# Column blocks of the input projection in parts of the tokens, with the convolution taken from the PSUM bank

## The chip, the cores and the metric

One core of a Trainium2 chip runs the whole layer as one program. The metric is the device time of one execution in microseconds. TensorE (PE) multiplies, VectorE (DVE), ScalarE (ACT) and GpSimd (POOL) do the elementwise work, SyncE (SP) issues most of the DMAs. Each engine takes its instructions in the order in which the program gives them; engines wait for each other by semaphores.

## The reference, cut to what matters

A layer normalises 1024 latent tokens (a grid of 16 rows by 64) and 256 context tokens, multiplies them by one input projection, and feeds the columns to a gated DeltaNet in two directions (queries, keys and values behind a short convolution) and to a pooling mixer. An output projection and a mixture of 16 experts follow. The part that the change touches:

```python
def short_conv(x, w):
    C = x.shape[-1]
    return lax.conv_general_dilated(
        x, w[:, None, :], window_strides=(1,),
        padding=[(CONV_K // 2, CONV_K - 1 - CONV_K // 2)],
        dimension_numbers=('NWC', 'WIO', 'NWC'), feature_group_count=C)
...
    proj = h @ w_in
    (q, k, v), log_a, beta = deltanet_inputs(proj[..., :QKV_COLS], proj[..., QKV_COLS:STATE_COLS],
                                             conv_w, a_log, dt_bias)
...
    feats = jax.nn.silu(short_conv(feat_pre, conv_w))
```

CONV_K is 4: token t of a channel sums tokens t-2, t-1, t and t+1 with weights 0 to 3, and tokens outside the sequence count as zero. Keys and values are computed for the context as well, queries, gates and pooled columns for the latent tokens alone.

## The kernel before

The projection is computed transposed, channels on the 128 partitions and tokens along the free axis, in column blocks of 128 channels: four key blocks, four value blocks, eight blocks that alternate between pooling and queries in the order PQ, four gate blocks. Inputs and weights are split into a high and a low float32r part (hx, hc for the tokens, whi, wlo for the weights), so that each k (8 slices of the 1024 inputs) takes three matmuls per tile. A block has the tiles px0 and px1 (512 latent tokens each, one PSUM bank each) and, for keys and values, pc (256 context tokens). Each of the names has one buffer in the PSUM pool PS2.

`project_steps` is a generator: for each k it issues the matmuls of all tiles of the block (six of 512 columns, and three of 256 with the context) and yields, eight times per block. At k = 1 it calls `prefetch`, which splits the next block's weights (ACT writes whi at L200, DVE or POOL writes wlo at L201; the first four on DVE) and has SP load the raw weights of the block after (L193, one buffer `wraw`).

After the block's last k a generator of its own, a post, is put into the list `posts`. `advance_posts` moves every post by one step. For keys, values and queries the post is `conv_post` (L407): in its first step ACT and DVE copy the PSUM tiles into `pad` and `padc` in SBUF; then ACT multiplies by the weight of tap 0 (L424) and, a step apart each, DVE adds the three other taps over all 1024 tokens (`scalar_tensor_tensor`, L428). The context's four taps follow in one step (L431, L433), then both Silus, and some steps later PE transposes the result in groups of four tiles of 128 tokens (L446). For keys ACT copies the group into `rows` and SP stores it (Kd); for values DVE scales it into `rows` (L463) and SP stores it (Vd). `rows` has one buffer, and so has `vT`, which holds a value block, a pooling block's input or, at first, the columns of a and beta.

The first key block is built while its inputs are still being modulated (L517 to L539); the three others run in a loop over `ks` (L584) that moves the posts and one step of the remaining small products of the modulation vector (`mg`, PE L132, fed by the DMA of `wm`) after each yield. The state of ten token chunks is then prepared by `prep` (L629), two chunks at a time, while values, queries, pooling and gates are projected: `run` (L782) calls `advance_preps` and `advance_posts` after each yield of the projection. A prep begins when every key block is through its transposes (`k_left`). It is a chain of small matmuls and short operations of DVE and ACT: kk (L663), eight products with the decays on DVE (L666), four transposes (L672), a first product on PE (L675), four rounds of PE (L687), DVE (L679, L683) and ACT (L681), then the joining of blocks (L700 to L743). Its masks are made by POOL, which also does the sums of the pooling posts (L821, L828). The scan over the chunks (`scan`, PE sc L923) begins when the projection and the last prep are through.

Of the kernel before, what the change touches and what calls it, by code (L numbers as in the profile page):

```python
# [52 lines left out]
def trunk_kernel(ctx, tc, x, c, ctxt, c_ctx, w_mod, b_mod, norm1, norm2, w_in, conv_w, a_log, dt_bias,  # L53
# [262 lines left out]
    def token_groups(n):  # L316
        return [(g, min(4, n - g)) for g in range(0, n, 4)]
# [88 lines left out]

    def conv_post(ct, px, pc, dst, after):  # L407

        pad = CV.tile([128, L + 4], F32, name="pad")
        acc = CV.tile([128, L], F32, name="acc")  # L410
        DVE.memset(pad[:, 0:2], 0.0)
        DVE.memset(pad[:, L + 2:L + 4], 0.0)
        for t in range(2):
            copy2(t, pad[:, 2 + 512 * t:514 + 512 * t], px[t])
        o = 0
        if pc is not None:
            padc = CV.tile([128, LC + 4], F32, name="padc")
            accc = CV.tile([128, LC], F32, name="accc")
            DVE.memset(padc[:, 0:2], 0.0)
            DVE.memset(padc[:, LC + 2:LC + 4], 0.0)  # L420
            ACT.activation(padc[:, 2:2 + LC], pc, AF.Copy)
            o = LC
        yield
        ACT.activation(acc, pad[:, 0:L], AF.Copy, scale=convw(0, ct))  # L424
        for j in range(1, 4):
            for _ in range(1):
                yield
            DVE.scalar_tensor_tensor(acc, pad[:, j:j + L], convw(j, ct), acc, op0=OP.mult, op1=OP.add)  # L428
        yield
        if pc is not None:  # L430
            DVE.tensor_scalar(accc, padc[:, 0:LC], convw(0, ct), None, op0=OP.mult)  # L431
            for j in range(1, 4):
                DVE.scalar_tensor_tensor(accc, padc[:, j:j + LC], convw(j, ct), accc, op0=OP.mult, op1=OP.add)  # L433
            ACT.activation(dst[:, 0:LC], accc, AF.Silu)
        ACT.activation(dst[:, o:o + L], acc, AF.Silu)
        yield
        for _ in range((1, 1, 0)[ct // 4]):
            yield
        n = (o + L) // 128
        tp = None  # L440
        for g, m in token_groups(n):
            if tp is not None:
                after(tp, *last)
            tp, last = rows_tile(ct, g // 4), (g, m)
            for q in range(m):
                PE.transpose(tp[:, q, :], dst[:, 128 * (g + q):128 * (g + q) + 128], ident)  # L446
            yield
        after(tp, *last)

    def k_sumsq(h):  # L450
        def f(tp, g, m):
            rows = CV.tile([128, 4, 128], F32, name="rows", bufs=1)
            ACT.activation(rows[:, :m], tp[:, :m], AF.Copy)
            SP.dma_start(Kd[g:g + m, :, h, :].rearrange("t p c -> p t c"), rows[:, :m])
            ACT.activation(tp[:, :m], tp[:, :m], AF.Square)
            DVE.tensor_reduce(ssk[:, g:g + m, h], tp[:, :m], axis=AX.X, op=OP.add)
            k_left[0] -= m
        return f

    def v_rows(h):  # L460
        def f(tp, g, m):
            rows = CV.tile([128, 4, 128], F32, name="rows", bufs=1)
# [13 lines left out]

    def project_tiles(with_ctx):
        return [(PS2.tile([128, 512], F32, name=f"px{t}"), hx, slice(512 * t, 512 * t + 512)) for t in range(2)] + \
            ([(PS2.tile([128, 512], F32, name="pc")[:, 0:LC], hc, slice(0, LC))] if with_ctx else [])

# [4 lines left out]

    def project_steps(n, with_ctx, post):
        for h in range(n):
            done[0] += 1
            hi, lo = split.pop(done[0] - 1)
            px = project_tiles(with_ctx)  # L490
            for k in range(KD):
                if k == 1:
                    prefetch()
                project_mm(px, k, ((hi, 0), (hi, 1), (lo, 0)), k == 0, k == KD - 1)
                if k == KD - 1:
                    posts.append(post(h, *project_out(px)))
                yield

    def project_out(px):
        return [p[0] for p in px[0:2]], px[2][0] if len(px) > 2 else None  # L500

# [4 lines left out]

    k_post = lambda h, px, pc: conv_post(4 + h, px, pc, kT[:, h, :], k_sumsq(h))
    mg = more_gemv()
    done[0] += 1
    hi, lo = split.pop(0)  # L510
    px = project_tiles(True)

# [27 lines left out]
    prefetch()  # L540
    first = project_out(px)
    ks = project_steps(H - 1, True, lambda h, px, pc: k_post(h + 1, px, pc))
    px, pc = ab_px[0:2], ab_px[2]
# [19 lines left out]
    def ab_post(px, pc):  # L563
        abT = CV.tile([128, LC + L], F32, name="vT")
        ACT.activation(abT[:, 0:LC], pc, AF.Copy)
# [15 lines left out]
    advance_posts()  # L581
    posts.append(k_post(0, *first))
    advance_posts()
# [205 lines left out]
    def v_post(h, px, pc):  # L789
        vT[0] = CV.tile([128, LC + L], F32, name="vT")  # L790
        return conv_post(8 + h, px, pc, vT[0], v_rows(h))

# [8 lines left out]

    def pool_post(g, px):

        w = 2 << g
        hw = w // 2
        wid = GRID + w
        u = CV.tile([128, LC + L], F32, name="vT").rearrange("p (r c) -> p r c", r=ROWS)
        s = PL.tile([128, ROWS + 16, GRID + 16], F32, name="psum_c")
        POOL.memset(u[:, :, 0:hw], 0.0)
        POOL.memset(u[:, :, hw + GRID:wid], 0.0)  # L810
        for t in range(2):
            copy2(t, u[:, 8 * t:8 * t + 8, hw:hw + GRID], px[t].rearrange("p (r c) -> p r c", c=GRID))
        POOL.memset(s[:, 0:hw, 0:GRID], 0.0)
# [34 lines left out]

    def gate_post(h, px):
        st = CV.tile([128, L + 4], F32, name="pad")[:, 0:L]  # L850
        for t in range(2):
            ACT.activation(st[:, 512 * t:512 * t + 512], px[t], AF.Silu)
        for _ in range(1):
            yield
        DVE.tensor_scalar(st, st, prmT[:, R_DN:R_DN + 1], None, op0=OP.mult)
        fp_store(h, st)

    def q_post(h, px):
        return conv_post(h, px, None, qT[:, h, :], q_sumsq(h))

    run(project_steps(2 * H, False,
                      lambda i, px, pc: (pool_post if PQ[i][0] == "p" else q_post)(PQ[i][1], px)))
    run(project_steps(H, False, lambda h, px, pc: gate_post(h, px)))
    while posts or todo or active:
# [986 lines left out]
```

## Time and profile before

| | us |
|---|---|
| time before, median of 3 runs | 1363.76 (1360.57 to 1364.97) |
| the profiled execution | 1365.92 |
| its span on the core | 1364.2 |
| PE busy | 1261.2 (92%) |
| DVE busy | 1029.5 (75%) |
| ACT busy | 751.1 (55%) |
| POOL busy | 390.6 (29%) |

The key blocks after the first take about us 69 to 140 of the span, the values to 234, queries and pooling to 430, the gates to 491. The scan, the output projection and the routing follow to about 782, the experts to the end. PE's busy time counts pipelined matmuls whose ends are modelled, so it doesn't show how many of them there could have been; its idle time, and what ended it, is a safer reading. An idle time in brackets stands at the instruction that ended it, with its releaser.

### The profile page before, as it was taken

Reading aid. Unit: us, or ns where it says so; the run is one execution under the profiler, and the core shown is the slowest. Engines: PE = TensorE matmul, PEld = TensorE weight load, DVE = VectorE, ACT = ScalarE, POOL = GpSimd, SP = SyncE. Lnnn points to the kernel's source line nnn. Section 1 sums busy time; section 2 is a strip of 40 time slices with the busy share of each in tenths; the row PEclk is TensorE's granted clock in tenths of the full one; section 3 lists DMA queues with packets and bytes.
Section 4 is the critical chain, followed back from the end, with each engine's and each line's share of the span. In section 5 each row is a group of like instructions: output and inputs, shape, how many; then the busy total and the mean of one; then the engine's idle time right before and its main releaser. Section 6 shows DMA issues by size and latency. Waiting matters only on the chain.

```text
span 1364.2 us, 26631 instructions
## 1 busy us (share of the span) xinstructions
PE 1261.2 (92%) x10355; PEld 1003.4 (74%) x10355; DVE 1029.5 (75%) x1773; ACT 751.1 (55%) x1103; POOL 390.6 (29%) x394
## 2 busy tenths in 40 slices
PE   5899889989999989989982799999999999999997
PEld 3476777666767779978872688888888888888884
DVE  4763665675775436864659699999999999999995
ACT  5443434343433324333233477777777777777783
POOL 5700552494865113761116000000000000000002
PEclk9999989998999989999995799999999999999999
DMA  9667213212123268634686599999999999999806
GB/s 353 209 193 276 70 37 91 86 49 79 49 79 95 87 221 317 214 128 154 231 322 232 188 340 369 386 385 384 379 383 382 388 381 385 383 382 383 298 4 259
DMA packets 140760, 328.39 MB, mean 241 GB/s; under 512 B 13517, under 2 KB 53082, under 8 KB 140634
## 3 DMA queue, kind: packets, MB, share of 16 engines
q1 hardware_dynamic: 134826, 305.72, 60.8%
q0 software_dynamic: 5376, 19.40, 5.6%
q8 instruction: 81, 1.33, 0.4%
q10 hardware_dynamic: 432, 1.57, 0.3%
q14 instruction: 45, 0.37, 0.1%
HBM read 287.32 MB, written 39.32 MB: 239 GB/s over the span
## 4 chain that ended last, share of the span: by engine, by line
PE 75%; DVE 11%; issue 4%; POOL 4%; DMA 3%; ACT 2%; SPq 0%; POOLq 0%; ACTq 0%; DVEq 0%
PE pg L1638 14%; PE pu L1638 13%; PE pd L1638 12%; PE px L484 11%; PE y L1256 6%; PE sc L923 5%; PE iv L687 2%; DVE acc L428 2%; PE tp L1674 2%; PE gv L132 1%; DMA wm<-in_w_mod_dram 1%; DVE pT L666 1%; DMA Vd<-rows 1%; PE pc L484 1%; DVE T L704 1%
## 5 line engine op out<-in xcount | busy, mean ns | idle before, releaser
L484 PE MATMUL px<-hx,whi 128*128 128x512 f32 x640 | 222.0, 427 | 4.6 <-ACT hx L290 2.7
L1516 DVE TENSOR_TENSOR flo<-rawb,fhi 128x1024 fp32r<-128x1024 f32 x176 | 208.6, 1224 | 11.2 <-ACT fhi L1515 10.5
L1515 ACT ACTIVATE fhi<-rawb 128x1024 fp32r<-128x1024 f32 x176 | 186.1, 1062 | 53.6 <-PE pg L1638 19.0
L1516 DVE TENSOR_TENSOR flo<-rawa,fhi 128x1024 fp32r<-128x1024 f32 x158 | 187.3, 1224 | 12.9 <-ACT fhi L1515 12.2
L1515 ACT ACTIVATE fhi<-rawa 128x1024 fp32r<-128x1024 f32 x158 | 167.2, 1062 | 51.3 <-PE pg L1638 21.9
L1638 PE MATMUL pg<-fhi,lhs 128*128 128x512 f32 x544 | 157.9, 402 | 0.0
L1638 PE MATMUL pu<-fhi,lhs 128*128 128x512 f32 x512 | 146.6, 398 | 0.0
L484 PEld LDWEIGHTS px<-hx,whi 128*128 128x128 f32 x640 | 113.2, 193 | 40.5 <-issue 12.4
L1744 POOL DMA_INDIRECT accd<-ye,ix x15 | 34.6, 2310 | 366.2 <-DVE ye L1742 366.2
L1638 PE MATMUL pd<-fhi,lhs 128*128 128x512 f32 x480 | 134.2, 396 | 0.0
L484 PE MATMUL px<-hx,wlo 128*128 128x512 f32 x320 | 128.5, 402 | 0.0
L1638 PEld LDWEIGHTS pg<-fhi,lhs 128*128 128x128 f32 x544 | 100.8, 190 | 22.6 <-ACT lhs L1676 0.4
L1638 PEld LDWEIGHTS pu<-fhi,lhs 128*128 128x128 f32 x512 | 95.1, 188 | 21.8
L1638 PEld LDWEIGHTS pd<-fhi,lhs 128*128 128x128 f32 x480 | 90.1, 188 | 21.6
L1638 PE MATMUL pg<-flo,lhs 128*128 128x512 f32 x272 | 86.2, 398 | 0.0
L1638 PE MATMUL pu<-flo,lhs 128*128 128x512 f32 x256 | 80.5, 395 | 0.0
L1256 PE MATMUL y<-ohi,mx 128*128 128x512 f32 x256 | 76.4, 404 | 0.8 <-DVE oa L981 0.8
L201 POOL TENSOR_TENSOR wlo<-wraw,whi 128x1024 fp32r<-128x1024 f32 x16 | 41.1, 2568 | 125.2 <-ACT whi L200 125.2
L1638 PE MATMUL pd<-flo,lhs 128*128 128x512 f32 x240 | 75.5, 396 | 0.0
L484 PEld LDWEIGHTS px<-hx,wlo 128*128 128x128 f32 x320 | 61.6, 193 | 14.0
L428 DVE SCALAR_TENSOR_TENSOR acc<-pad,prmT,acc 128x1024 f32<-128x1024 f32 x36 | 66.3, 1843 | 3.6 <-ACT acc L424 3.3
L1664 POOL DMA_INDIRECT xe<-h2d,ix x16 | 16.4, 1027 | 168.7 <-PE pg L1638 120.7
(453 smaller groups left out, 2405.1 us busy)
## 6 DMA issues: line engine op xcount, KB each, us to landing
rawb<-in_w_down_dram SPq DMA_DIRECT2D x61, 512.0 KB, 6.1
rawb<-in_w_gate_dram SPq DMA_DIRECT2D x58, 512.0 KB, 5.1
rawb<-in_w_up_dram SPq DMA_DIRECT2D x57, 512.0 KB, 6.0
rawa<-in_w_gate_dram SPq DMA_DIRECT2D x56, 512.0 KB, 5.0
rawa<-in_w_up_dram SPq DMA_DIRECT2D x54, 512.0 KB, 6.1
rawa<-in_w_down_dram SPq DMA_DIRECT2D x52, 512.0 KB, 6.1
wm<-in_w_mod_dram SPq DMA_DIRECT2D x48, 512.0 KB, 5.7
wraw<-in_w_in_dram SPq DMA_DIRECT2D x20, 512.0 KB, 4.1
```

Source lines behind the costliest of these rows:

```text
L201: (POOL if pos[0] > 4 else DVE).tensor_tensor(lo[:, :, :n], raw[:, :, :n], hi[:, :, :n].bitcast(F32), op=OP.subtract)
L428: DVE.scalar_tensor_tensor(acc, pad[:, j:j + L], convw(j, ct), acc, op0=OP.mult, op1=OP.add)
L484: PE.matmul(dst, wp[:, k, :], src[hp][:, k, o], start=start and i == 0, stop=stop and i == len(parts) - 1)
L687: PE.matmul(iv[r, u, o:64], pa[r, u, :], PV[r, u, o:64], start=True, stop=True)
L923: PE.matmul(p[:, h, :], lhs(h), rhs(h), start=True, stop=True)
L1256: PE.matmul(ys[t, hf][:, hf, :], l_[:, k, :], r_[:, 512 * hf:512 * hf + 512], start=(k == KORD[0] and i == 0), stop=(k == KORD[-1] and i = ...
L1515: ACT.activation(hi, raw, AF.Copy)
L1516: (eng or DVE).tensor_tensor(lo, raw, hi.bitcast(F32), op=OP.subtract)
L1638: PE.matmul(ps[:, hf, :], l_[:, k, :], r_[:, 512 * hf:512 * hf + 512], start=(k == 0 and n == 0), stop=(k == KD - 1 and n == 2))
L1664: POOL.indirect_dma_start(out=xe[e], out_offset=None, in_=h2d[:, :], in_offset=bass.IndirectOffsetOnAxis(ap=ix[:, 0:1], axis=0))
L1674: PE.transpose(tp[:, q, :], src[:, 128 * k:128 * k + 128], ident)
L1744: POOL.indirect_dma_start(out=accd[:, :], out_offset=bass.IndirectOffsetOnAxis(ap=idx.pop(e)[:, 0:1], axis=0), in_=ye, in_offset=None, com ...
```

## The change

A block is now computed part after part: context (for keys and values), then the first 512 latent tokens, then the second, each over all eight k before the next part begins. The tile `px` has two buffers, which the parts take in turn. A part of 512 tokens yields four times, after six matmuls each; the context part yields twice, after twelve. A block with the context therefore has ten steps where it had eight.

Each part has its own post, put into the list after its last k. `conv_part` does the convolution without the copies: ACT writes tap 2 from the PSUM tile to the place of the result, and DVE adds the taps 0, 1 and 3 in place, reading the same PSUM tile, a step apart (the context's three in one step). The two tokens at the seam between the parts get a small operation of their own. The PSUM tile is free when tap 3 is done. `pad`, `acc`, `padc` and `accc` go; one Silu in place takes context and latent tokens together. `rows` and `vT` get two buffers. The posts of pooling and gates take parts as well; the gates write to a tile `gt`.

```diff
-    def conv_post(ct, px, pc, dst, after):
...
+    def conv_part(ct, acc, b, ps):
+
+        n, e = ps.shape[1], acc.shape[1]
+        h = 2 if b else 0
+        if b + n < e:
+            DVE.memset(acc[:, b + n:b + n + 2], 0.0)
+        ACT.activation(acc[:, b + h:b + n], ps[:, h:n], AF.Copy, scale=convw(2, ct))
+        if h:
+            DVE.scalar_tensor_tensor(acc[:, b:b + 2], ps[:, 0:2], convw(2, ct), acc[:, b:b + 2], op0=OP.mult, op1=OP.add)
+        for j in (0, 1, 3):
+            if n > LC or j == 0:
                 yield
-            DVE.scalar_tensor_tensor(acc, pad[:, j:j + L], convw(j, ct), acc, op0=OP.mult, op1=OP.add)
-        yield
...
+            t0, t1 = max(b + 2 - j, 0), min(b + n + 2 - j, e)
+            DVE.scalar_tensor_tensor(acc[:, t0:t1], ps[:, t0 + j - 2 - b:t1 + j - 2 - b], convw(j, ct), acc[:, t0:t1],
+                                     op0=OP.mult, op1=OP.add)
+        yield
+
+    def conv_post(ct, dst, after, part, ps):
+
+        n = dst.shape[1]
+        o = n - L
+        if part == "c":
+            yield from conv_part(ct, dst[:, 0:LC], 0, ps)
+            return
+        yield from conv_part(ct, dst[:, o:n], 512 * part, ps)
+        if part == 0:
+            return
+        ACT.activation(dst, dst, AF.Silu)
         yield
...
-            rows = CV.tile([128, 4, 128], F32, name="rows", bufs=1)
+            rows = CV.tile([128, 4, 128], F32, name="rows", bufs=2)
...
+    def project_tile(part):
+        if part == "c":
+            return PS2.tile([128, 512], F32, name="pc")[:, 0:LC], hc, slice(0, LC)
+        return PS2.tile([128, 512], F32, name="px", bufs=2), hx, slice(512 * part, 512 * part + 512)
...
+            for part in ("c", 0, 1)[0 if with_ctx else 1:]:
+                tile = project_tile(part)
+                for k in range(KD):
+                    if k == 1 and part == ("c" if with_ctx else 0):
+                        prefetch()
+                    project_mm([tile], k, ((hi, 0), (hi, 1), (lo, 0)), k == 0, k == KD - 1)
+                    if k == KD - 1:
+                        posts.append(post(h, part, tile[0]))
+                    if k % 4 == 3 or part != "c" and k % 2:
+                        yield
...
-    px = project_tiles(True)
+    px = [project_tile(part) for part in (0, 1, "c")]
...
-    posts.append(k_post(0, *first))
+    for part, ps in zip((0, 1, "c"), first):
+        posts.append(k_post(0, part, ps))
...
+        if part == "c":
+            vT[0] = CV.tile([128, LC + L], F32, name="vT", bufs=2)
+        return conv_post(8 + h, vT[0], v_rows(h), part, ps)
...
+    def gate_post(h, part, ps):
+        if part == 0:
+            gate_t[h] = CV.tile([128, L], F32, name="gt")
+        st = gate_t[h]
+        ACT.activation(st[:, 512 * part:512 * part + 512], ps, AF.Silu)
+        yield
+        if part == 0:
+            return
```

## Rows read from the trace of the kernel before

**Rows 1.** Busy time by stage; the first row names the columns.

```profile
core 0: us, PE busy (x) PEld busy (x) DVE busy (x) ACT busy (x) POOL busy (x), PEclk, DMA share, GB/s
...
69.00:140.00 71.00, 69.86 (x421) 47.70 (x420) 33.44 (x92) 30.44 (x51) 6.69 (x6) 1.00 0.67 225
...
140.00:234.00 94.00, 84.75 (x1151) 71.50 (x1150) 60.79 (x126) 36.83 (x64) 41.01 (x31) 0.95 0.22 65
...
234.00:430.00 196.00, 183.78 (x3144) 138.71 (x3142) 127.72 (x260) 75.01 (x144) 125.72 (x92) 0.95 0.24 73
```

**Rows 2.** Waits, us 140 to 491: waiter, releaser, us in total, times, longest.

```profile
PE iv L675 <- DVE PV L672: 8.0, 7, 5.7
...
PE iv L728 <- DVE T L722: 7.0, 4, 2.8
...
PE iv L687 <- DVE PV L683: 4.6, 5, 1.9
...
PE iv L728 <- ACT T L731: 1.3, 1, 1.3
...
PE iv L700 <- DVE PV L692: 0.2, 1, 0.2
...
ACT vT L434 <- DVE accc L433: 18.5, 3, 11.7
```

**Rows 3.** One source line each: count, ns min/median/max, first and last start.

```profile
L428 DVE SCALAR_TENSOR_TENSOR acc<-pad,prmT,acc x36: 1272/1285/4329, 76.4 to 400.7; 128x1024 f32<-128x1024 f32 x36
...
L666 DVE SCALAR_TENSOR_TENSOR pT<-dt,nbt,pT x80: 335/341/351, 170.3 to 465.4; 128x128 f32<-128x128 f32 x80
...
L1780 DVE SCALAR_TENSOR_TENSOR ye<-pg,af,g2b x2: 741/746/750, 1336.8 to 1337.5; 128x512 f32<-128x512 f32 x2
...
L433 DVE SCALAR_TENSOR_TENSOR accc<-padc,prmT,accc x24: 483/485/488, 82.4 to 249.5; 128x256 f32<-128x256 f32 x24
```

**Rows 4.** Timeline: start us, duration, engine, operation, idle time in brackets.

```profile
166.31 4.08 DVE L428 SCALAR_TENSOR_TENSOR acc<-pad,prmT,acc 128x1024 f32<-128x1024 f32 x2
...
173.07 0.68 PE L675 MATMUL iv<-PV,pT 32*32 32x32 f32 x4 [5.71 <-DVE PV L672]
...
278.57 17.61 POOL L828 TENSOR_TENSOR psum_c<-psum_c 128x1984 f32<-128x1984 f32 x4
...
279.83 4.33 DVE L428 SCALAR_TENSOR_TENSOR acc<-pad,prmT,acc 128x1024 f32<-128x1024 f32 x1 [1.64 <-ACT acc L424]
```

**Rows 5.** Timeline of DVE and PE at the last value block.

```profile
238.30 0.42 DVE L463 TENSOR_TENSOR rows<-tp,nrk 128x256 f32<-128x256 f32 x1 [3.38 <-DMA Vd<-rows]
...
241.25 0.93 PE L728 MATMUL iv<-T,pT 64*64 64x64 f32 x16 [2.80 <-DVE T L722]
```

**Rows 6.** First of five low-clock windows, and their sum; columns as in Rows 1.

```profile
170.50:180.70 10.20, 7.22 (x137) 5.83 (x137) 6.21 (x18) 1.64 (x3) 7.53 (x2) 0.50 0.01 3
...
sum 30.70, PE 27.00 PEld 18.87 DVE 20.94 ACT 5.22 POOL 12.44; mean PE 5.40 PEld 3.77 DVE 4.19 ACT 1.04 POOL 2.49
```

**Rows 7.** From the first key block to the second: timelines, landing of wraw.

```profile
66.78 9.72 SPq L193 DMA_DIRECT2D wraw<-in_w_in_dram  x2
...
DMA to landing us min/median/max: 3.9/3.9/3.9
...
68.78 0.39 ACT L421 ACTIVATE padc<-pc 128x256 f32<-128x256 f32 x1 [0.78 <-PE pc L484]
...
74.88 1.22 DVE L201 TENSOR_TENSOR wlo<-wraw,whi 128x1024 fp32r<-128x1024 f32 x1 [5.23 <-ACT whi L200]
```

**Rows 8.** Waits of PEld, 69 to 140; chain of waits, 142 to 150.

```profile
PEld gv L132 <- DMA wm<-in_w_mod_dram: 5.3, 6, 1.2
...
146.94 1.40 PE px L484 x6
```

**Rows 9.** Timeline at the end of the projection.

```profile
492.14 1.36 POOL L890 DMA_DIRECT2D v<-Vd  x2 [17.59 <-PE iv L728]
...
495.79 2.05 PE L923 MATMUL sc<-v,T 128*128 128x128 f32 x8 [0.43 <-DMA v<-Vd]
```

More of the change, by code (lines that the diff above doesn't have):

```diff
@@ L438, in conv_post @@
             yield
-        n = (o + L) // 128
         tp = None
-        for g, m in token_groups(n):
+        for g, m in token_groups(n // 128):
             if tp is not None:
@@ L461, in f @@
         def f(tp, g, m):
-            rows = CV.tile([128, 4, 128], F32, name="rows", bufs=1)
+            rows = CV.tile([128, 4, 128], F32, name="rows", bufs=2)
             DVE.tensor_tensor(rows[:, :m], tp[:, :m], nrk[:, g:g + m, h:h + 1].to_broadcast([128, m, 128]),
@@ L540, in trunk_kernel @@
     prefetch()
-    first = project_out(px)
-    ks = project_steps(H - 1, True, lambda h, px, pc: k_post(h + 1, px, pc))
+    first = [p[0] for p in px]
+    ks = project_steps(H - 1, True, lambda h, part, ps: k_post(h + 1, part, ps))
     px, pc = ab_px[0:2], ab_px[2]
@@ L563, in ab_post @@
     def ab_post(px, pc):
[L564 removed]
+        abT = CV.tile([128, LC + L], F32, name="vT", bufs=2)
         ACT.activation(abT[:, 0:LC], pc, AF.Copy)
@@ L787, in trunk_kernel, with v_post @@
     vT = [None]
-    def v_post(h, px, pc):
-        vT[0] = CV.tile([128, LC + L], F32, name="vT")
-        return conv_post(8 + h, px, pc, vT[0], v_rows(h))
+    def v_post(h, part, ps):
+        if part == "c":
+            vT[0] = CV.tile([128, LC + L], F32, name="vT", bufs=2)
+        return conv_post(8 + h, vT[0], v_rows(h), part, ps)
     run(project_steps(H, True, v_post))
@@ L800, in fp_store, with pool_post @@
         SP.dma_start(fpd[:, :, i, :].rearrange("t p c -> p t c"), src.rearrange("p (t c) -> p t c", c=128))
-    def pool_post(g, px):
+    pool_u = {}
+    def pool_post(g, part, ps):
         w = 2 << g
@@ L806, in pool_post @@
         wid = GRID + w
-        u = CV.tile([128, LC + L], F32, name="vT").rearrange("p (r c) -> p r c", r=ROWS)
+        if part == 0:
+            pool_u[g] = CV.tile([128, LC + L], F32, name="vT", bufs=2).rearrange("p (r c) -> p r c", r=ROWS)
+            POOL.memset(pool_u[g][:, :, 0:hw], 0.0)
+            POOL.memset(pool_u[g][:, :, hw + GRID:wid], 0.0)
+        u = pool_u[g]
+        copy2(part, u[:, 8 * part:8 * part + 8, hw:hw + GRID], ps.rearrange("p (r c) -> p r c", c=GRID))
+        if part == 0:
+            return
         s = PL.tile([128, ROWS + 16, GRID + 16], F32, name="psum_c")
[L809 to L812, printed above, removed]
         POOL.memset(s[:, 0:hw, 0:GRID], 0.0)
@@ L847, in pool_post, with q_post @@
         fp_store(H + g, m)
[L849 to L854, printed above, removed]
+    gate_t = {}
+    def gate_post(h, part, ps):
+        if part == 0:
+            gate_t[h] = CV.tile([128, L], F32, name="gt")
+        st = gate_t[h]
+        ACT.activation(st[:, 512 * part:512 * part + 512], ps, AF.Silu)
+        yield
+        if part == 0:
+            return
         DVE.tensor_scalar(st, st, prmT[:, R_DN:R_DN + 1], None, op0=OP.mult)
         fp_store(h, st)
-    def q_post(h, px):
-        return conv_post(h, px, None, qT[:, h, :], q_sumsq(h))
+    def q_post(h, part, ps):
+        return conv_post(h, qT[:, h, :], q_sumsq(h), part, ps)
     run(project_steps(2 * H, False,
-                      lambda i, px, pc: (pool_post if PQ[i][0] == "p" else q_post)(PQ[i][1], px)))
-    run(project_steps(H, False, lambda h, px, pc: gate_post(h, px)))
+                      lambda i, part, ps: (pool_post if PQ[i][0] == "p" else q_post)(PQ[i][1], part, ps)))
+    run(project_steps(H, False, gate_post))
     while posts or todo or active:
```

39 lines of the change are left out of this document (1 added, 38 removed).

## The prediction

> **What bounds the kernel now.** I read the profile in this order: busy time by stage, to see where the changed code runs; the waits of PE in that stretch; the instructions that PE waited for; then what had delayed those.
>
> The changed code runs from us 69 to 491. PE is taken as busy nearly all of the key stage, 69.9 of 71 us, and is idle more in the two stages behind it, 9.3 of 94 us and 12.2 of 196 us [rows 1]. So no matmul is saved by the change, and none is: what it can give back are waits. In us 140 to 491 PE waited 23.3 us in nine groups; the first four are 20.9 us, the last is 0.2 us, and all four are first matmuls of a prep step that wait for DVE or ACT [rows 2]. The matmuls of the projection themselves wait for almost nothing: between the end of a block and the next stand prep matmuls that hide the copies.
>
> What had delayed DVE is the convolution. A tap over 1024 tokens takes 1.285 us at the median and up to 4.33 us [rows 3]. The long ones lie beside POOL: the tap at 279.83 took 4.33 us while POOL ran four sums from 278.57 on [rows 4]. Two taps from 166.31 on take 4.08 us, where two medians are 2.57, and behind them PE idles 5.71 us for the first prep [rows 4]. DVE's 80 operations of the same kind that read one operand from PSUM run in the same stretch and never leave 335 to 351 ns [rows 3]. So it is the pair DVE and POOL, both on SBUF, that is slow, not the operation.
>
> Two more costs follow. With the single `rows` DVE waits for the store of the group before: 3.38 us at 238.30, behind which PE idles 2.80 us [rows 5]. And five stretches between us 170 and 410, 30.7 us in all, run at a granted clock of 0.50, which is the 1.2 GHz level; the first begins in the 5.71 us idle time. PE is busy 27.0 us of them [rows 6], so at 2.4 GHz it would have needed about 13.5 us less.
>
> **The change part by part.** The sum is made against the profiled execution: 1365.9 us, of which the span is 1364.2 and 1.7 lie around it; the median of the runs is 2.2 us lower.
>
> *Taps from PSUM.* Removed are 36 taps of 1024 tokens, the copies and the separate tap 0; added are 72 taps of 512. The nearest row is the same operation of 512 elements from PSUM late in the kernel: 746 ns [rows 3]. Six of them are 4.48 us per block, where three old ones are 3.86 us at the median and 12.99 us at the worst [rows 3]. So DVE has no less work where POOL is quiet; the gain is that a queue of 1.3 to 4.3 us in front of a prep step becomes 0.75 us. Taken wait by wait [rows 2]: the first prep's 5.7 us had 4.08 us of taps ahead of it and keeps one of 0.75, so 3.3 go. Of the 4.6 us of the rounds (L687) nearly all lies behind single long taps: 4.0 go. The 1.3 us for ACT comes of a Silu that waited in ACT's queue for the context's taps; ACT waited 18.5 us in all for those, which now end a part earlier: 1.0 goes. Of the other 2.3 us of L675 1.0 goes, of the 4.2 us of L728 that are not the store's 1.4, of the 2.4 us of small ones 1.2. Sum: 11.9 us. It can't be more than the 20.5 us that are not the store's. It can be nothing if the prep's own chain, eight decay products and four transposes, is what is late next.
>
> The Trainium skill speaks against this part: "VectorE: DVE Perf Modes", section "Rules for kernel authors", has a kernel that does many operations on a matmul's output copy it to SBUF first. By it the old form would be the right one, and two taps of 0.746 against one of 1.285 us [rows 3] agree with it as long as POOL is quiet; what it would make of the time is the second rival.
>
> *Two buffers for rows and vT.* The wait of 2.80 us [rows 5] nearly goes: 2.5 us. SP's queue has the same stores in the same order, none is added.
>
> *The clock.* If the idle times in front of the stretches shrink, the stretches do. Of the 13.5 us I take 9, the share of the waits that go, with 0 and 13.5 as ends.
>
> *The first key block.* Here the change adds a wait. All three parts of that block go into `posts` together, and the second block now begins with its context part, whose tile pc has one buffer: its first matmul waits until the context's taps of the first block are done. In DVE's queue stand in front of these: the split of the third block's low weights (`prefetch` is now issued before the posts move), one reduction, and one tap of each part of 512. The split waits for ACT, and ACT for `wraw`, which SP issues at 66.78 and which lands 3.9 us later, at 70.7 [rows 7]. From there: about 1.0 us of ACT for whi, 1.22 us for wlo [rows 7], about 0.4 for the reduction, 2 x 0.746, and 3 taps of 256 at 0.485 or so [rows 3]: 5.5 us, so 76.2. PE is ready when the old copy of the context begins, 68.78 [rows 7]. Queued behind that matmul on PE are the transposes of a and beta and the small products: nothing else can run, and PE idles about 7 us (4 to 9). After the 5.71 us idle time PE ran at half speed for several us [rows 4, 6]; I take 4 us for that. The first latent part then waits for tap 3 of the first block, behind the reductions that need those transposes: 2 us more. Against these 13 us stands that the small products have waited up to 5.3 us for their weights [rows 8], whose loads go on meanwhile: 4 us come back. Net 9 us lost, with 3 and 15 as ends.
>
> *Steps.* Blocks with context have ten steps for eight. A step of six matmuls is 1.40 us [rows 8], so twelve of 256 columns are about as long. The four value blocks give the preps eight steps more, and the first prep begins one step earlier, so the preps end some nine steps ahead of the last matmul. Today the load of the first scan's `v`, issued on POOL's queue, waits for the last prep (492.14) and the scan for that load (495.79) [rows 9]. I take 2 us for it, 0 to 5: SP's loads for the second chunk stay where they are.
>
> *A PSUM tile that is held longer.* Until tap 3 is done, three steps after ACT's read. The part that needs the tile begins a whole step later, with 1.40 us of matmuls [rows 8] and a prep step in between. Tap 3 stands on DVE behind that step's prep operations. I take 1.5 us, 0 to 20.
>
> *At no cost:* the seam operation and the fewer memsets (two columns each, DVE is free over a third of these stages [rows 1]); the gates' Silu by halves and a few more loads of ACT's tables (ACT is busy 75 of 196 us [rows 1]); if that cover went it would be a microsecond per gate block. Everything behind the scan's start moves as a whole.
>
> Sum: -11.9 - 2.5 - 9 + 9 - 2 + 1.5 = -14.9 us, so 1351.0 for the profiled execution and about 1349 for the median.
>
> **The rivals.** *First, the first key block costs little* (the loads are ahead, or the clock does not fall) and the clock comes back in full: -11.9 - 2.5 - 13 + 4 - 2 = -25, so 1339. For it: all waits of the list have a tap or a store ahead of them. Against: `wraw` is issued only when the split before it has read the buffer [rows 7].
>
> *Second, the taps bring no relief.* Behind them the prep's own chain or POOL's sums end last; only the store, the scan's start and about 2 us of clock are gained: -2.5 - 2 - 2 + 9 = +2.5, so 1366. The rule of the Trainium skill named above would have it so. For it: the waits of L728, 7.0 us [rows 2], have the decay products in front of them anyway. Against: the steady 341 ns beside POOL [rows 3].
>
> *Third, slower: PE waits for its PSUM tile.* If DVE is more than one step behind when it reaches tap 3, each such part begins late. Ten preps have one step in which DVE has the eight products and four transposes to do, 8 x 0.341 us [rows 3] and the transposes, some 4 us, against a step of 1.40 us of matmuls [rows 8] and a prep product of about 0.93 [rows 5]; 2 us each are 20 us, and with no clock gained: -11.9 - 2.5 + 9 - 2 + 20 = +12.6, so 1376. It decides from a queue on DVE longer than one step. Against it: a prep step waits for the same DVE queue before PE reaches the tile.
>
> **How the numbers follow.** Forecast 0.52 (1341 to 1358), first rival 0.14, second 0.20, third 0.14. A measurement here can't tell less than 0.3%, about 4 us, from no change. Faster by more, below 1359.7: 0.50 + 0.14 + 0.06 = 0.70. Within: 0.02 + 0.12 + 0.02 = 0.16. Slower: 0.02 + 0.12 = 0.14. The range 1336 to 1367 leaves out part of the first rival (0.05) and nearly all of the third with some of the second (0.16).
>
> **What would show it.** Right: taps of about 0.75 us with a narrow spread, also beside POOL; PE's waits in the prep stages down from 23 to about 9 us; an idle time of about 7 us at the second key block, ended by DVE; the key stage some 9 us longer and the stages behind it together some 22 us shorter; no wait of DVE for a store of Vd. Wrong: matmuls of px waiting for a tap in most blocks, taps that still stretch beside POOL, or as much time at 1.2 GHz as before.

## The result and the profile after

The changed kernel takes 1347.26 us (median of 4 runs, 1346.57 to 1351.26), the kernel before 1362.45 us in the same comparison (4 runs, 1360.57 to 1364.97). The ratio is 0.9893 with a 95% interval of 0.9866 to 0.9921: 15.2 us faster, where 14.9 were forecast. The profiled execution took 1351.26 us, its span 1349.5 us.

The total came out almost exactly. Its terms did not all: the second buffer for `rows`, taken away again, was worth some 7 us more than forecast; the stages behind the keys, where taps and clock were to gain, were shortened by some 7 us less than forecast; and some 6 us came behind the scan's start, where none were forecast.

Busy time by stage of the kernel after, cut at the same blocks as in [rows 1]; columns as there:

```profile
69.00:149.00 80.00, 71.03 (x426) 50.27 (x427) 38.69 (x98) 30.97 (x52) 8.80 (x11) 0.94 0.60 204
149.00:246.00 97.00, 92.00 (x1484) 74.50 (x1483) 57.73 (x142) 39.13 (x69) 33.30 (x25) 0.96 0.23 70
246.00:434.00 188.00, 179.68 (x3154) 137.49 (x3153) 120.01 (x263) 74.73 (x145) 117.67 (x93) 0.98 0.24 73
434.00:485.00 51.00, 50.27 (x768) 38.15 (x766) 17.76 (x50) 16.43 (x37) 12.74 (x14) 1.00 0.37 115
```

The key stage has grown from 71 to 80 us and PE is idle 9.0 us in it, where it was idle 1.1. The three stages behind it (values, queries and pooling, gates) take 336 us where they took 351 [rows 1 gives the first two]. The value stage looks 3 us longer only because its blocks have ten steps and take in more of the preps (1484 matmul records for 1151); the last stage is shorter for the same reason (768 for 1093).

Waits of PE, first in the key stage (us 60 to 150), then behind it (us 140 to 478): waiter, releaser, us in total, times, longest.

```profile
PE pc L483 <- DVE kT L420: 6.7, 1, 6.7
PE px L483 <- DVE kT L420: 2.3, 1, 2.3
...
PE iv L728 <- DVE T L722: 4.6, 4, 1.2
PE iv L739 <- DVE pa L734: 3.6, 3, 2.7
PE iv L675 <- DVE PV L672: 2.3, 5, 1.5
PE dt L663 <- ACT pT L647: 1.3, 1, 1.3
PE iv L728 <- ACT T L731: 0.7, 1, 0.7
PE iv L687 <- DVE PV L683: 0.6, 1, 0.6
PE pc L850 <- DVE pm L852: 0.4, 1, 0.4
```

In the prep stages 13.5 us are left of 23.3 [rows 2]. Against [rows 2]: L675 went from 8.0 to 2.3, L687 from 4.6 to 0.6, L728 from 7.0 to 4.6, and a wait that was not among the larger ones before, L739, takes 3.6. No matmul of px waits for a tap anywhere but at the second key block.

The taps of the kernel after (source line 420: count, ns min/median/max, first and last start), and one of the two POOL products beside them (line 607):

```profile
L420 DVE SCALAR_TENSOR_TENSOR kT<-px,prmT,kT x24: 736/743/751, 72.7 to 151.4; 128x512 f32<-128x512 f32 x12, 128x511 f32<-128x511 f32 x8, 128x510 f32<-128x510 f32 x4
L420 DVE SCALAR_TENSOR_TENSOR qT<-px,prmT,qT x24: 734/746/753, 275.7 to 399.7; 128x512 f32<-128x512 f32 x12, 128x511 f32<-128x511 f32 x8, 128x510 f32<-128x510 f32 x4
...
L607 POOL TENSOR_TENSOR rh<-mi,lah x20: 1039/1040/1042, 135.0 to 408.6; 128x512 fp32r<-128x512 f32 x20
```

This answers to [rows 3]: 1285 ns with a tail to 4329 has become 743 to 746 with no tail, also among the queries, where POOL sums. POOL's products on line 607 are as steady, at 1.04 us, where the longest took 2.09 us before.

Stretches at 1.2 GHz in us 69 to 485, two in the key stage and two behind it, against five behind it in [rows 6]; columns as in Rows 1:

```profile
73.10:79.90 6.80, 4.27 (x20) 3.59 (x24) 2.79 (x7) 0.00 (x0) 0.00 (x0) 0.50 0.30 78
86.70:90.10 3.40, 3.40 (x12) 2.71 (x11) 1.48 (x6) 2.20 (x2) 0.00 (x0) 0.50 0.35 130
172.00:178.80 6.80, 6.42 (x133) 4.90 (x134) 4.50 (x10) 0.38 (x1) 6.80 (x3) 0.50 0.01 2
294.90:301.80 6.90, 6.67 (x87) 5.34 (x88) 2.24 (x6) 4.05 (x6) 6.82 (x3) 0.51 0.01 4
```

Behind the key stage 13.7 us are left of 30.7, with PE busy 13.1 of them where it was 27.0: half of the difference, about 7 us, is what the clock gave back there in this pair of executions.

The added wait, and the end of the projection, in PE's timeline (start us, duration, operation, idle time in brackets):

```profile
75.63 0.77 PE L483 MATMUL pc<-hc,whi 128*128 128x256 f32 x2 [6.69 <-DVE kT L420]
...
85.67 0.74 PE L483 MATMUL px<-hx,whi 128*128 128x512 f32 x2 [2.34 <-DVE kT L420]
...
148.54 0.39 PE L483 MATMUL px<-hx,wlo 128*128 128x512 f32 x1
...
484.67 0.39 PE L483 MATMUL px<-hx,wlo 128*128 128x512 f32 x1
485.75 1.16 PE L911 MATMUL kq<-qT,kT 128*128 128x128 f32 x8 [0.69 <-ACT gt L861]
486.74 1.95 PE L933 MATMUL sc<-v,T 128*128 128x128 f32 x16
```

The key stage's last matmul starts at 148.5 (before: 139.4), the projection's at 484.7 (before: 490.3), the scan 2.0 us behind it (before, from [rows 9], at 495.79, 5.5 us behind). So the span's 14.7 us are made up of +9.1 in the key stage, -14.7 behind it, -3.5 at the scan's start and -5.6 later on.

### The profile page after: what moved, and what is told of

Read it like the earlier page. It is cut to its first block, busy times and chain, and to the rows that moved or that the text cites. A ratio compares the mean times of both kernels' runs of the same rounds, so it can differ in the third digit from the quotient of the medians.

```text
span 1349.5 us, 26618 instructions
## 1 busy us (share of the span) xinstructions
PE 1251.2 (93%) x10355; PEld 996.5 (74%) x10355; DVE 1011.1 (75%) x1773; ACT 748.8 (55%) x1097; POOL 371.1 (27%) x394
## 4 chain that ended last, share of the span: by engine, by line
PE 81%; DVE 8%; POOL 4%; issue 3%; ACT 2%; DMA 1%; SPq 0%; POOLq 0%; ACTq 0%; DVEq 0%
PE px L483 15%; PE pg L1648 14%; PE pu L1648 13%; PE pd L1648 12%; PE y L1266 6%; PE sc L933 5%; PE iv L687 3%; PE tp L1684 2%; PE gv L132 1%; PE pc L483 1%; DVE pT L666 1%; DVE PV L672 1%; PE tp L444 1%; PE iv L739 1%; POOL oraw L1060 1%
## 5 line engine op out<-in xcount | busy, mean ns | idle before, releaser
L483 PE MATMUL px<-hx,whi 128*128 128x512 f32 x640 | 218.7, 421 | 5.8 <-ACT hx L290 2.8
L483 PEld LDWEIGHTS px<-hx,wlo 128*128 128x128 f32 x320 | 60.9, 190 | 13.6
L1648 PEld LDWEIGHTS pg<-flo,lhs 128*128 128x128 f32 x272 | 51.5, 189 | 12.2
```

What stands on the lines that cost most here:

```text
L483: PE.matmul(dst, wp[:, k, :], src[hp][:, k, o], start=start and i == 0, stop=stop and i == len(parts) - 1)
L1648: PE.matmul(ps[:, hf, :], l_[:, k, :], r_[:, 512 * hf:512 * hf + 512], start=(k == 0 and n == 0), stop=(k == KD - 1 and n == 2))
```

## The experiments

The time of a kernel is its median beside that of the kernel before on the same chip; "after" stands for the 1347.26 above. The kernel before took 1361.6 to 1363.9 us on these chips, so two changed kernels are compared more safely by their ratios.

| kernel | us | ratio to before, 95% |
|---|---|---|
| after | 1347.26 | 0.9893 (0.9866 to 0.9921) |
| e1_ctx_done | 1342.11 | 0.9850 (0.9815 to 0.9885) |
| e2_ctx_split | 1346.43 | 0.9890 (0.9857 to 0.9924) |
| e8_all_taps | 1339.67 | 0.9834 (0.9808 to 0.9860) |
| e4_sbuf_taps | 1377.97 | 1.0121 (1.0087 to 1.0156) |
| e7_steps8 | 1345.16 | 0.9873 (0.9839 to 0.9908) |
| e9_all_taps_steps8 | 1338.26 | 0.9825 (0.9794 to 0.9856) |
| b_nosums | 1354.01 | 0.9942 (0.9924 to 0.9960) |
| a_nosums | 1342.61 | 0.9866 (0.9840 to 0.9891) |
| b_rows2 | 1352.58 | 0.9931 (0.9907 to 0.9954) |
| a_rows1 | 1357.95 | 0.9956 (0.9939 to 0.9972) |
| a_rowk1 | 1358.00 | 0.9970 (0.9951 to 0.9988) |
| a_rowv1 | 1349.11 | 0.9929 (0.9903 to 0.9955) |

**The first key block.** *e1_ctx_done* runs the context's convolution of the first block at once, ahead of the loop over the steps:

```diff
-    for part, ps in zip((0, 1, "c"), first):
+    for part, ps in zip((0, 1), first):
         posts.append(k_post(0, part, ps))
     advance_posts()
+    for _ in k_post(0, "c", first[2]):
+        pass
```

> The changed kernel with one move: the context post of the first key block is run to its end before the loop over the other key blocks, so that its three taps stand on DVE ahead of the split of the third block's weights. My theory (the key stage is 9 us longer because the second block waits for these taps): the context is read by ACT until about 69.1 and three taps of 0.48 us follow, so PE waits 1.5 to 2 us instead of 6.7, the stretch at the lower clock behind it shrinks, and the time is 1338 to 1343 against 1347 of the changed kernel. Rival (the key stage is set by the loads of the small products' weights, and the wait only hides them): the end of the fourth key block stays at about 148.5 us and the time at 1347.

1342.11 us, 5 us below after. The wait at the second block's first matmul is 1.9 us instead of 6.7 and ends with ACT's whi; the second wait, 2.3 us, is unchanged. The theory held.

*e2_ctx_split* adds to e1 that the split of the third block's weights is issued in the first latent part and not in the context part:

```diff
-                    if k == 1 and part == ("c" if with_ctx else 0):
+                    if k == 1 and part == ("c" if with_ctx and done[0] != 2 else 0):
                         prefetch()
```

> As the kernel before it, and the split of the third block's weights is issued at k = 1 of the second block's first latent part instead of its context part, so that the latent taps of the first block are not behind it either. My theory: the second wait (2.3 us, first latent part on tap 3 of the first block) goes as well, 1336 to 1341. Rival: that wait hangs on the reductions that need PE's transposes and not on the split; then the time is that of the kernel before it, within 2 us.

1346.43 us, which neither the theory nor the rival had: the second wait did not go, it doubled to 4.7 us. DVE's timeline ahead of the tap that ends it (first e1, then e2):

```profile
77.41 0.29 DVE L573 TENSOR_REDUCE ab<-ab 128x32 f32<-128x128 f32 x1 [1.27 <-PE ab L571]
...
78.91 1.41 DVE L420 SCALAR_TENSOR_TENSOR kT<-px,prmT,kT 128x511 f32<-128x511 f32 x2
```

```profile
77.93 1.23 DVE L201 TENSOR_TENSOR wlo<-wraw,whi 128x1024 fp32r<-128x1024 f32 x1 [3.18 <-ACT whi L200]
79.07 0.28 DVE L573 TENSOR_REDUCE ab<-ab 128x32 f32<-128x128 f32 x1
...
80.57 1.41 DVE L420 SCALAR_TENSOR_TENSOR kT<-px,prmT,kT 128x511 f32<-128x511 f32 x2
```

In both the last tap stands behind a reduction that needs PE's transposes, and behind small operations for masks; e2 has put the split, with 3.18 us of waiting for ACT, in front of it as well. So the second wait is not the split's; it comes of the tap's place in DVE's queue.

*e8_all_taps* therefore issues all taps of the first block, the latent parts' too, ahead of the loop:

```diff
+    first_posts = [k_post(0, part, ps) for part, ps in zip((0, 1, "c"), first)]
+    posts.extend(first_posts[:2])
     advance_posts()
+    for _ in first_posts[2]:
+        pass
+    for _ in range(3):
+        for g in first_posts[:2]:
+            next(g)
```

> The changed kernel, but the first key block's context post is run to its end and its two latent posts through their last taps ahead of the loop over the other key blocks, so that all nine taps stand on DVE ahead of the third block's weight split and of the reductions. Theory after the first runs (both waits at the second key block are the place of these taps in DVE's queue; the second hangs on the reductions, since moving the split behind it made it longer, 4.7 us): no wait of 2.3 us is left, one of about 2 us at most stays, and the time is 1338 to 1341. Rival (once the taps are out of the way the loads of the small products' weights end last): the waits for those loads come back and the time stays at 1342.

1339.67 us, 7.6 below after. Of the two waits one of 1.9 us is left, and the last matmul of the key stage starts at 139.25, as before the change. So the first block cost the change about 8 us, and nearly all of it is the place of these taps.

**Where the taps read.** *e4_sbuf_taps* copies each latent part (the first key block's apart) from PSUM to SBUF with ACT and lets the taps read the copy:

```diff
         ACT.activation(acc[:, b + h:b + n], ps[:, h:n], AF.Copy, scale=convw(2, ct))
+        if ct != 4 and n > LC:
+            sb = CV.tile([128, L], F32, name="gt")[:, 0:n]
+            ACT.activation(sb, ps, AF.Copy)
+            ps = sb
```

> The changed kernel, but each latent part (the first key block's excepted, so that the wait at the second block stays) is copied by ACT to SBUF first, and the three taps read the copy. Parts, steps, two-buffered tiles and order stay. My theory (the gain comes of taking one operand from PSUM, out of POOL's way): the taps of 512 take about 0.7 us where POOL is quiet and up to 4 beside it, PE's waits in the prep stages rise by 4 to 8 us, and the time is 1352 to 1358. Rival (the gain comes of the shorter pieces spread over more steps): 1345 to 1349, with the taps' median alone changed.

1377.97 us, 31 us above after and 16 above before: the direction was the theory's, the size three times as much. Its taps by form (line 424), and the two largest waits of PE in us 150 to 510:

```profile
L424 DVE SCALAR_TENSOR_TENSOR vT<-gt,prmT,vT x24: 702/745/2749, 160.5 to 258.7; 128x512 f32<-128x512 f32 x12, 128x511 f32<-128x511 f32 x8, 128x510 f32<-128x510 f32 x4
L424 DVE SCALAR_TENSOR_TENSOR qT<-gt,prmT,qT x24: 742/1456/4041, 282.3 to 424.1; 128x512 f32<-128x512 f32 x12, 128x511 f32<-128x511 f32 x8, 128x510 f32<-128x510 f32 x4
...
PE iv L743 <- DVE pa L738: 10.3, 4, 5.7
PE iv L732 <- DVE T L726: 9.3, 5, 2.4
```

Among the queries, where POOL sums, the same 512-element tap takes 742 to 4041 ns with its input in SBUF, 1456 at the median; from PSUM it took 734 to 753. So it is the place of the input that makes the tail. How much of the 31 us is that tail is not told apart: the edit also adds 22 copies of 0.59 us on ACT, through one buffer, and DVE waits for them.

**The POOL sums.** *b_nosums* (of the kernel before) and *a_nosums* (of after) leave the pooling's sums out:

```diff
-        POOL.memset(s[:, 0:hw, 0:GRID], 0.0)
-        POOL.memset(s[:, hw + ROWS:w + ROWS, 0:GRID], 0.0)
+        POOL.memset(s[:, 0:ROWS, 0:GRID], 1.0)
...
-            POOL.tensor_tensor(dst, src[:, :, 0:n], src[:, :, sh:sh + n], op=OP.add)
...
-            POOL.tensor_tensor(s[:, 0:n, 0:GRID], s[:, 0:n, 0:GRID], s[:, sh:sh + n, 0:GRID], op=OP.add)
```

> The kernel before, with POOL's pooling sums left out (the tile of sums is filled with ones instead); the steps, the copies and DVE's part of the pooling stay. This kernel leaves out part of the computation. Theory (taps that share SBUF with POOL's sums are what PE waited for among the queries): the taps of the query blocks fall from up to 4.3 us to 1.3 or at most 2.6, PE's waits for L683 and the stretches at the lower clock there go, and the time falls by 6 to 10 us to 1352 to 1356. Rival (the prep's own chain is what PE waited for): within 3 us of 1362.

> The changed kernel, with POOL's pooling sums left out in the same way. This kernel leaves out part of the computation. Theory (its taps are out of POOL's way, and only the prep's and the pooling's own operations with two operands in SBUF still meet the sums, as the identity addition of 3.95 us at 290 us): a smaller gain than in the kernel before, 2 to 5 us, 1342 to 1345. Rival (the sums cost both kernels the same): 6 to 10 us, 1337 to 1341.

Before gains 7.7 us by it (1354.01 against 1361.67), after 4.7 (1342.61; 3.7 by the ratios, whose intervals overlap). What changed in each is in its waits of PE (b_nosums, us 140 to 491; then a_nosums, us 140 to 480):

```profile
PE iv L728 <- DVE T L722: 7.9, 4, 3.0
PE iv L675 <- DVE PV L672: 7.3, 7, 5.7
...
PE iv L687 <- DVE PV L683: 0.7, 1, 0.7
```

```profile
PE iv L728 <- DVE T L722: 4.7, 4, 1.3
PE iv L675 <- DVE PV L672: 2.3, 5, 1.5
...
PE iv L687 <- DVE PV L683: 0.8, 2, 0.6
```

The sums carried L687 before (4.6 to 0.7) and L739 after (3.6 to none). The sums are not the whole of POOL: the 5.7 us of the first prep and the 7.9 us of L728 stay without them, as the first collision of [rows 4], at 166.31, lies before the pooling begins. Among the queries, too, one tap of b_nosums still took 3.41 us, more than the 2.6 expected.

Why after still gains by it is in the timelines of DVE, POOL and PE of after:

```profile
290.14 3.95 DVE L676 TENSOR_TENSOR PV<-PV,id 128x256 f32<-128x256 f32 x1
...
289.63 4.17 POOL L834 TENSOR_TENSOR psum_c<-psum_c 128x1856 f32<-128x1856 f32 x1
...
295.13 1.60 PE L739 MATMUL iv<-T,pa 64*64 64x64 f32 x16 [2.68 <-DVE pa L734]
```

An operation of the prep itself, with both inputs in SBUF, takes 3.95 us beside a sum, where its minimum is 424 ns in the same kernel; PE idles 2.68 us behind it, and the low-clock stretch at 294.90 begins there. The change took the taps out of the collision, not the prep.

**Steps.** *e7_steps8* takes the two additional steps per value block away from the preps:

```diff
-    def run(steps):
-        for _ in steps:
-            advance_preps()
+    def run(steps, skip=()):
+        for i, _ in enumerate(steps):
+            if i % 10 not in skip:
+                advance_preps()
...
-    run(project_steps(H, True, v_post))
+    run(project_steps(H, True, v_post), (0, 1))
```

> The changed kernel, but the preps are not moved in the two context steps of a value block, so that a value block moves them eight times, as the old kernel did. My theory (the preps' earlier end lets the first scan's loads go ahead of the last matmul): the last prep ends within one or two steps of the last projection matmul, the scan begins 4 to 5 us behind that matmul instead of 2, and the time is 1349 to 1353. Rival (PE is the bound and the order of preps is worth nothing): 1347 within 2 us.

1345.16 us, if anything 2 us less, and the scan still begins 2.0 us behind the projection's last matmul (478.16 and 480.23). So the additional moves of the preps, by which I had explained the gain at the scan's start, are worth nothing. What they were to bring is there without them: in e7 POOL issues the load of the scan's `v` 4.5 us ahead of the projection's last matmul (in after at 472.01, 12.7 us ahead), where before it was issued behind that matmul, at 492.14 [rows 9]:

```profile
473.66 1.07 POOL L901 DMA_DIRECT2D v<-Vd  x2 [17.13 <-PE iv L728]
```

*e9_all_taps_steps8* is e7 on top of e8:

> As the kernel before it, with the preps not moved in the context steps of the value blocks. Theory (the moves of the preps in those steps bring nothing, and a little is lost since a step of twelve short matmuls covers no more than one of six): 2 us less than the kernel before it, 1336 to 1339. Rival (the 2 us between the two kernels with and without these moves were chance): the same as the kernel before it.

1338.26 us, 23 below before and the fastest of all; against e8 it is 1.4 us, less than can be told.

**The second buffer for rows.** *b_rows2* gives the kernel before two buffers for `rows`, *a_rows1* takes the second from after, both in `k_sumsq` and `v_rows`:

```diff
-            rows = CV.tile([128, 4, 128], F32, name="rows", bufs=1)
+            rows = CV.tile([128, 4, 128], F32, name="rows", bufs=2)
```

> The kernel before with two buffers for rows and nothing else. Theory (a wait of DVE for a store, and the 2.8 us that PE idles behind one of them with 3.4 us at the lower clock after it): DVE's 12.0 us of waits for stores go, PE's wait of 2.80 us becomes one of under 1 us, and the time falls by 2.5 to 4 us, to 1358 to 1360. Rival (the wait is taken up elsewhere, since the prep behind it has its own chain): within 1 us of 1362.

> The changed kernel with one buffer for rows again and nothing else. Theory: the waits of DVE for the stores of Vd come back, some 10 us on DVE, and PE idles 2 to 4 us more behind them: 1349 to 1352 against 1347. Rival (with ten steps per value block the groups are further apart and the store is done in time): 1347 within 1 us.

Both missed in size. b_rows2 is 11.3 us faster than before (1352.58 against 1363.87), a_rows1 10.7 slower than after; by the ratios 9 us each. I had said 2.5. The second buffer of `vT` was not taken away by itself. In a_rows1 the key stage's last matmul starts at 154.92 for 148.54, so 6.4 us are lost where I had counted nothing. SP's timeline there, of after, and then of a_rows1 with the rows of ACT and PE that belong to it:

```profile
101.30 1.47 SPq L452 DMA_DIRECT2D Kd<-rows  x2
102.85 2.19 SPq L122 DMA_DIRECT2D wm<-in_w_mod_dram  x4
```

```profile
101.32 5.84 SPq L452 DMA_DIRECT2D Kd<-rows  x2
107.25 2.15 SPq L122 DMA_DIRECT2D wm<-in_w_mod_dram  x4
...
106.39 0.38 ACT L451 ACTIVATE rows<-tp 128x256 f32<-128x256 f32 x1 [4.60 <-DMA Kd<-rows]
...
114.65 1.05 PE L132 MATMUL gv<-wm,cs 128*32 128x512 f32 x4 [0.31 <-DMA wm<-in_w_mod_dram]
```

The chain: ACT waits 4.60 us until the store before has read `rows`; the next store, already issued on SP, waits for ACT; and the loads of `wm` behind it in SP's order, which need neither, start 4.4 us later. PE then waits for them at the small products, 2.5 us in all in six places, and the weight loads another 6.0.

*a_rowk1* and *a_rowv1* give one buffer to the keys' rows alone and to the values' rows alone, by putting them into the gates' tile `gt`, which has one. In `k_sumsq` (for a_rowk1) or `v_rows` (for a_rowv1):

```diff
-            rows = CV.tile([128, 4, 128], F32, name="rows", bufs=2)
+            rows = CV.tile([128, L], F32, name="gt")[:, 0:512].rearrange("p (t c) -> p t c", c=128)
```

> The changed kernel with one buffer for the keys' rows (the free tile of the gates is used for it) and two for the values'. Theory (the key blocks' stores are what the second buffer was worth: with one, ACT and the store on SP's queue wait, the weight loads of the small products stand behind that store and come 4 to 6 us late, and PE waits for them): the key stage ends at about 155 us instead of 148.5, the time is 1353 to 1357 against 1347 of the changed and 1358 of the kernel with one buffer for both. Rival (the values' stores are): 1347 to 1350.

> The changed kernel with one buffer for the values' rows and two for the keys'. Theory (as in the kernel before it): the key stage ends at 148.5 us, DVE waits some 5 us for the stores of Vd, the value stage is 1 to 3 us longer, the time 1348 to 1351. Rival: 1354 to 1358.

The keys' buffer is worth 10.7 us (1358.00), the values' 1.9 (1349.11, with an interval that overlaps the one of after). With one buffer for the keys the loads of wm start at 106.28 again, late as in a_rows1, and the key stage's last matmul starts at 154.25 for 148.54. The traces place these 5.7 us of the 10.7; where the rest lies they do not show. The value stores, the only ones I had costed, are the small part.

In the kernel before the second buffer does something else as well. There b_rows2 ends the key stage only about 1.6 us earlier. Its low-clock stretches behind it are these, 17.0 us against the 30.7 of [rows 6]:

```profile
167.00:177.20 10.20, 6.97 (x137) 5.73 (x137) 6.45 (x19) 1.64 (x3) 7.78 (x2) 0.51 0.01 2
279.70:283.10 3.40, 3.40 (x46) 2.59 (x36) 3.40 (x2) 0.00 (x0) 3.32 (x2) 0.53 0.00 0
395.60:399.00 3.40, 3.40 (x6) 2.08 (x7) 3.00 (x7) 0.00 (x0) 0.00 (x0) 0.51 0.02 5
```

PE is busy 13.8 us in them for 27.0, some 6.6 us at full speed, and PE's waits there are 19.3 us for 23.3. With the 1.6 us these are 12 of the 13.6 us between the two profiled executions (1365.92 and 1352.34 us; the medians differ by 9 to 11). Its taps were even slower than before (median 1708 ns, maximum 4335), and it still gained. That the buffer itself took the low-clock stretches away is not shown: in the changed kernel taking it out did not bring them back (10.2 us behind the keys in a_rows1, 13.7 in after).

## Why the prediction was right, and where it was not

**Right in sum, by errors that cancel.** The kernel after without the second buffer (a_rows1) is 5.9 us faster than before, 6.0 by the ratio; the buffer adds 9 to 11. The prediction had the buffer at 2.5 and all the rest at 12.4. The stages of the two profiled executions say the same: the key stage came as forecast, the stages behind it fell 7 us short of the forecast 22, and 5.6 us behind the scan's start, with 1.5 more at it, made up for them. That the sum came out within 0.3 us is luck.

**Two buffers for rows: -2.5 forecast, -9 to -11 measured.** The step that failed: I priced the wait in [rows 5] and said of SP's queue that it has the same stores in the same order, none added. DVE's waits for the stores of Vd went as forecast, and the values' buffer, which is what I had priced, measured 1.9. The rest is true and beside the point: the order is the cost. A store that waits for its producer held the loads behind it, by 4.4 us in a_rows1. The view that hints at it was open: in the kernel before ACT waits for the keys' stores too, in us 80 to 160 (waiter, releaser, total, times, longest):

```profile
ACT rows L453 <- DMA Kd<-rows: 7.2, 4, 3.4
```

I had read the stores' waits in the value stage alone, as PE waited there. In the kernel before these waits cost the key stage little (b_rows2 ends it 1.6 us earlier); in the changed one they cost 6.4 us.

**Taps and clock: -11.9 and -9 forecast.** The mechanism held in every part: taps at 0.743 us with no tail, also beside POOL; L675 and L687 nearly gone; fewer stretches at 1.2 GHz. The sizes were too large. In a_rows1, which has one buffer for `rows` as before, the stages behind the keys take 337.4 us (154.92 to 492.28) where they took 350.9: 13.5 us gained, where 11.9 + 9 - 1.5 = 19.4 were forecast. In after, waits of PE fell by 9.8 us, where taps and store together were to give 14.4; the clock gave 7 us. That last number is one pair of executions'. Behind the keys the traces of the ten kernels whose taps read PSUM have between none (a_nosums) and 13.7 us (after) at 1.2 GHz, those of the three kernels with the old taps and of e4 17.0 (b_rows2 and b_nosums) to 30.7 (before). So the place of the taps goes with the clock; how much a single buffer or wait does to it these traces do not tell. What was missed in the waits: L739 is new, since `PV<-PV,id` meets the sums as the taps had done, and L728 kept 4.6 us. The forecast had named that end ("the prep's own chain ... is what is late next") only as the case in which nothing is gained; it took about a third.

With the second buffer the stages behind the keys were to be 22 us shorter and are 14.7. Waits and clock give 9.8 + 7 = 16.8 of them; the 2 us lost against that are not settled.

**The first key block: +9 forecast, +9.1 measured.** The parts came near to what was worked out, one of them for another reason. The first matmul starts at 75.63 (forecast 76.2), after 6.7 us (7); the second wait is 2.3 us (2); PE is busy 7.7 us at 1.2 GHz, which is 3.8 us more than at 2.4 (4); and the weight loads' 5.3 us of waiting for wm [rows 8] are gone (4 forecast). These make 7.5 us; 1.6 are not placed. e8 moves the taps ahead, and 7.6 us go. But the weight loads' waits went only with the second buffer, and not because the loads had more time: in a_rows1, with the same idle time of PE, they are 6.0 us, PE waits 2.5 for the same loads, and the key stage ends 15.5 us later than before. So the 4 us that were to come back here are a part of what the buffer is worth.

**The scan's start: -2 forecast, -3.5 measured, not by the additional steps.** The scan follows the projection by 2.0 us for 5.5, and as forecast the load of `v` no longer comes behind the last matmul. But e7 shows that the additional steps are not needed for it. That the first prep begins one step earlier is one thing that is left; that alone was not tried.

**A PSUM tile held longer: +1.5 forecast, none seen.** In no block but the second does a matmul of px wait for a tap, so the third rival fell whole.

**The second rival** (the taps bring no relief) fell with e4. The rule of the Trainium skill behind it, "VectorE: DVE Perf Modes", section "Rules for kernel authors", to copy first if many operations follow (it lets the kernel read PSUM otherwise), gave a kernel 31 us slower here, of which the copies themselves have a share that was not measured. What fits the rows is another page of the Trainium skill, "SBUF — State Buffer", section "Who interferes with whom": an operation of DVE with two SBUF inputs contends with a GpSimd one that reads SBUF, one with at most one SBUF input, outside VectorE's 2-port modes, does not. The traces agree with both halves: 734 to 753 ns from PSUM, 742 to 4041 from SBUF, in the same stage.

**Not forecast: -5.6 us behind the scan's start.** In the scan's first part before runs at 1.2 GHz for 10.3 us, after for 3.4:

```profile
494.70:501.60 6.90, 6.03 (x28) 5.50 (x27) 0.00 (x0) 0.00 (x0) 1.49 (x2) 0.51 1.05 368
505.00:508.40 3.40, 3.40 (x16) 3.40 (x17) 0.00 (x0) 2.40 (x11) 0.87 (x1) 0.50 1.04 383
```

```profile
492.90:496.30 3.40, 3.40 (x18) 3.40 (x17) 0.98 (x2) 2.32 (x11) 0.00 (x0) 0.50 1.02 369
```

PE is busy 9.4 us there before and 3.4 after, so about 3 us are the clock's. The other stretches at 1.2 GHz behind the scan's start are shorter too: 6.8 us from 607.4 and 54.6 from 713.2 before, 3.4 from 595.3 and 51.2 from 701.1 after. The two long ones (before, then after):

```profile
713.20:767.80 54.60, 18.14 (x85) 15.27 (x86) 43.81 (x185) 15.59 (x45) 25.48 (x20) 0.50 0.56 193
```

```profile
701.10:752.30 51.20, 16.54 (x81) 14.01 (x82) 42.37 (x182) 13.24 (x42) 23.70 (x20) 0.50 0.56 196
```

In all these PE is busy 33.9 us before and 23.2 after; half of the difference is 5.3 us, so nearly all of the 5.6 is the clock's. The other traces agree: from the scan's start to the end before and b_nosums take 868.4 and 868.8 us, with 71.7 us at 1.2 GHz from the end of the projection on; b_rows2 865.0 with 64.9; after 862.8 with 58.0; a_rowv1 861.2 with 54.6. What makes the stretches shorter is open. The idle time ahead of the scan does not settle it: b_rows2, whose scan begins 5.6 us behind the projection as before, runs only 3.4 us at 1.2 GHz at the scan's start.

Open, too, is what sets the spread of some kernels (the ten runs of a_rowk1 lie between 1352.8 and 1359.0), beside which differences of 2 us say little.

## What to carry to other kernels

When a buffer is doubled, price the whole queue behind the transfer that waits for it, not only the wait of its producer: here one more buffer for `rows`, above all the keys', was worth 9 to 11 us, more than the 6 us that all the rest of the change gave net. Where VectorE and GpSimd work side by side, let VectorE read one input from PSUM, and look for the other operations with two SBUF inputs, which inherit the collision. And where a change frees a tile only at the end of a post, run the first block's post ahead of the loop: that is the step from 1347 to 1340 us.

## What the runs showed of the hardware

In the collision of VectorE and GpSimd a short operation lasted almost as long as the other's long one: one that takes 424 ns at the least took 3.95 us beside a GpSimd sum of 4.17 us. So it doesn't need many operations to matter: around the end of PE's idle time behind it (2.68 us) 6.9 us at 1.2 GHz began. And the time at 1.2 GHz has to be counted beside the waits: the execution of b_rows2 has 4 us less of PE's waits than that of before, and 13.7 us less at 1.2 GHz, but a difference of that kind between two executions is not yet the work of the one thing that was changed.
